# A decoder block on one core: the attention gate's modulation sums in an earlier stage, latent kv and q by token tile and half, and q's squares summed on ScalarE

## The chip, the core and the metric

The kernel runs on one core of a Trainium2 chip. The core has TensorE (PE, matrix products, with its weight loads as PEld), VectorE (DVE), ScalarE (ACT), GpSimd (POOL), SyncE (SP, which issues most loads), and 16 DMA engines. Each engine takes its instructions in the order in which the built program has them. The metric is the time of one execution on the device, in microseconds, the median of several runs.

## What is computed

One hybrid decoder block on 512 tokens of 1024 channels, in float32. A conditioning vector c gives six modulation vectors; h is the normed and modulated input; one wide product with `w_in` feeds two attention branches (latent attention, MLA, and native sparse attention, NSA) and two merge gates; then a merge, an output product and a SwiGLU mixer.

```
mod = silu(c) @ ada_w + ada_b                      # six vectors of 1024
sh1, sc1, gt1, sh2, sc2, gt2 = split(mod, 6)
h = rms_norm(x, norm1_gain) * (1 + sc1) + sh1
z = h @ w_in                                       # c_q, c_kv, k_pe, q_n, k_c, v_c, ..., gates
q  = rms_norm(c_q, q_a_gain) @ w_q_b               # 768 -> 8 heads x 96
kv = rms_norm(c_kv, kv_a_gain) @ w_kv_b            # 256 -> 8 heads x (64 + 64)
q, k = rms_norm over each head's 96, rope on the last 32
y_mla = causal_attention(q, k, v) @ w_o_mla
y_nsa = nsa_attention(...) @ w_o_nsa
x = x + gt1 * ((sigmoid(g_mla) * y_mla + sigmoid(g_nsa) * y_nsa) @ w_out)
h2 = rms_norm(x, norm2_gain) * (1 + sc2) + sh2
x = x + gt2 * ((silu(h2 @ w_gate) * (h2 @ w_up)) @ w_down)
```

The attention branch's gate modulation is gt1.

## The kernel before, in words

**Products in pieces.** A float32 product is made of three faster ones: each operand is split into a high and a low part (`hi_of` on ScalarE, `lo_of` on VectorE or GpSimd), and high x high, high x low and low x high are added in PSUM. A slab of weights goes through `wchunk`: a load by SP into `raw`, then `whi` on ScalarE and `wlo` on VectorE, four buffers of each.

**Stages.** The times are those of the profile, from the span's start. First `first_gemm`: it sums the modulation of sh1 and sc1 from strips of `ada_w` (tile `araw`), transposes and modulates x, and multiplies the first columns of `w_in` (to about 61 us). Then `segb2` (`gemm_wide`, eight slabs of 536 columns, tiles wa and wb) and `sega` (three `gemm_tok` of 352 columns, tile ga) multiply the next columns (to about 152). Beside them `weave` sets `prep`, a chain of small steps: q and k of the sparse branch are normed, turned and split (UQ, UK, sqq, pq, pk), and its compressed keys are made (X, FF, FS, cmp_w). Then the sparse attention (to about 290), with the merge gates' products (tile gp) as filler; then the stage here called the head projection (about 292 to 350); then the loop over the eight MLA heads (to about 447), then `y_mla`, the output product and the mixer.

**The head projection.** `latent_cols` transposes the latent rows in zA into cT, in a high and a low part. Two `gemm_tok` of `w_kv_b` (tile gk, 512 columns each, four heads a half) and two of `w_q_b` (tile gq, 384 columns) follow. `gemm_tok` holds the four token tiles in four PSUM buffers and finishes all of them at its end; the next one reuses the four. `use_kv` squares, copies and splits; the last token tile of a half norms k. `use_q` squares a tile on ScalarE into jq, copies it to qn, ropes it on VectorE, and sums jq's squares there by a reduction to msq. `norm_q` turns msq into the scale rsq, its iterations on GpSimd.

**The heads.** `mla_heads` transposes one head of qn and kn (tile pt) and splits them into qh, ql, kh, kl. `mla_scores` makes four score tiles ps (two PSUM buffers) and reduces each on VectorE, with the row minimum mn; ScalarE takes the exponential; VectorE scales. `mla_values` transposes the probabilities s, splits them into phi and plo, and multiplies with VM into av.

**Later modulations.** `mods` is a generator for gt1, sh2, sc2 and gt2. A half (512 channels) takes four strips of 512 KB; each strip's load is one step, and its two sums on VectorE (macc; the first of a half is a plain product) the next. So a half is eight steps. The half before is finished some steps later: two row halves of gt1 and gt2 by a product with ones (tile pm), a bias loaded into the row (gt), an addition, and for gt1 a halving on ScalarE. A strip lies in a buffer of `raw`, or, if `strip_src` holds a pool, in that pool's one buffer `strip`. `Side` hands out steps: eight in the head projection (`E_MODS`) and eight in the head loop (`F_MODS`), sixteen in all, then more in the stages behind.

**Who sets the order.** The program text gives an order, a scheduler at build time moves instructions of each engine where dependences allow it, and `pace` and `gate` add a few orders for fillers. So the engines' order of before and after is read from the built programs.

Of the kernel before, what the change touches and what calls it, by code (L numbers as in the profile page):

```python
# [28 lines left out]
WARM = 18  # L29
BRIDGE = 6  # L30
# [12 lines left out]
E_MODS = 8  # L43
F_MODS = 8
# [71 lines left out]
def hybrid_block(ctx, tc, a, out):  # L116
# [481 lines left out]
    w_in = a["w_in"][0]  # L598
    tab_st = scope()
# [338 lines left out]
    def latent_stats(pool_):  # L938
        for t in range(NT):
# [19 lines left out]
    segb2 = gemm_wide(hA, w_in, KD, SEG_B + 768, 280, 256, use_w, use_s, pair_first=True)  # L959
    pq, pk = prep_q(), prep_k()  # L960
    K, V = (0, "k"), (1, "v")
    prep = chain(compress_blocks(*K), part(pq, 5), compress_w1(*K), part(pq, 4), compress_w2(*K), compress_blocks(*V),
                 compress_out(*K), pq, compress_w1(*V), part(pk, 5), compress_w2(*V), pk, compress_out(*V), prep_gates())
    weave(segb2, prep, 1, 1)
    sega = chain(*[gemm_tok(hA, w_in, KD, SEG_A + c0, 352, use_a(c0), tag=f"a{c0}") for c0 in (0, 352, 704)])
    weave(sega, prep, 2, 1)
    run(prep)
    cp_st.close()
    zb_st.close()

    spilled = [dr.tile([4, P, S], F32, name=f"spill{i}") for i in range(6)]

    def turned_mm(ps, cols, A, h, l, first, last):
        for i, o in enumerate(ps):
            c = slice(cols + i * P, cols + (i + 1) * P)
            pe.matmul(o, h[:, c], A[0], start=first, stop=False)
            pe.matmul(o, h[:, c], A[1], start=False, stop=False)
            pe.matmul(o, l[:, c], A[0], start=False, stop=last)

    spill_src = {}  # L980

    def spill(ps, at, gate=None):
        if "pool" in spill_src:
            gs = spill_src["pool"].tile([P, S], F32, name="gs", tag="gs", bufs=spill_src["bufs"])
        else:
            gs = wp.tile([P, 1024], F32, name="gs", tag="raw")[:, :S]
        if gate is None:
            act.activation(out=gs, in_=ps, func=AF.Tanh, scale=0.5)
            act.dma_start(out=spilled[at // 4][at % 4], in_=gs)
        else:  # L990
            dve.scalar_tensor_tensor(out=gs, in0=gate, scalar=1.0, in1=ps, op0=ALU.add, op1=ALU.mult)
            pool.dma_start(out=spilled[at // 4][at % 4], in_=gs)

    def ahead(jobs, lead=1, eng=lambda: ()):
        ready = [wchunk(*job, *eng()) for job in jobs[:lead]]
        for i in range(len(jobs)):
            if i + lead < len(jobs):
                ready.append(wchunk(*jobs[i + lead], *eng()))
            yield ready.pop(0)

    def gates():
        jobs = [(rows(w_in, 0, KD, SEG_C + c, P), KD, P) for c in range(0, 2 * D, P)]
        for i, (h, l) in enumerate(ahead(jobs, FILL_LEAD, fill_lo)):
            ps = mm.tile([P, S], F32, name="gp", tag="mm")
            for k in range(KD):
                turned_mm([ps], 0, hT[k], h[:, k, :], l[:, k, :], k == 0, k == KD - 1)
                if k == KD - 1:
                    spill(ps, i)
                yield

    def y_nsa():
        jobs = [(rows(a["w_o_nsa"][0], 0, 4, c, 256), 4, 256) for c in range(0, D, 256)]
        for i, (h, l) in enumerate(ahead(jobs, FILL_LEAD, fill_lo)):
# [814 lines left out]
```

## Time and profile before

| | |
|---|---|
| median of three runs | 881.77 us (880.79 to 883.82) |
| the profiled execution's own time | 879.25 us |
| its span, first to last instruction | 877.5 us |
| mean granted TensorE clock | 0.989 |
| busy: PE, PEld, DVE, ACT, POOL | 842.3, 739.0, 677.2, 454.2, 122.0 us |
| DMA moved | 115.53 MB, mean 132 GB/s |

The profile is of one execution. A row of the windows gives a stretch, its length, then for PE, PEld, DVE, ACT and POOL the busy time and in brackets the number of instructions, the granted TensorE clock, the mean busy share of the DMA engines, and GB/s. A row of the waits names who waited for whom, the total, the number of times and the longest. A row of the timeline gives start, length, engine, operation, result and operands, shape and count, and in square brackets the idle time ahead of it and what ended that. Line 152 is that of a helper through which all engines' calls pass, so the rows are told apart by tile names. The end of a matrix product is modelled and products overlap, so starts are compared with starts.

### The profile page before, as it was taken

How to read it: one execution, taken by the hardware profiler on the slowest of the kernel's cores; microseconds unless marked ns; L12 is line 12 of the kernel's file. 1: busy time of each engine (PE TensorE's matmuls, PEld its weight loads, DVE VectorE, ACT ScalarE, POOL GpSimd, SP SyncE). 2: the span in 40 equal slices, each digit the busy share in tenths (PEclk: the TensorE clock that was granted, in tenths of full speed). 3: DMA queues.
4: the chain of work that ended last, by engine and by line, in shares of the span. 5: the costliest groups of instructions: out<-in, count | busy, mean ns of one | idle time of the engine just before them, and what ended most of it. 6: DMA issues, size and time to landing. Idle time of an engine off the chain costs nothing.

```text
span 877.5 us, 13876 instructions
## 1 busy us (share of the span) xinstructions
PE 842.3 (96%) x5028; PEld 739.0 (84%) x5028; DVE 677.2 (77%) x1400; ACT 454.2 (52%) x906; POOL 122.0 (14%) x203
## 2 busy tenths in 40 slices
PE   8899999889999998899899999999999999999997
PEld 6789899668777697688688889898999889988996
DVE  5788796887876689578879876986887759865875
ACT  4646564786765655466534264542465326641550
POOL 0005145343432025012200000000000000000000
PEclk9999999999999999799999999999999999999999
DMA  9944554221102456126497752453233413333312
GB/s 311 301 145 135 162 146 125 61 73 37 61 12 70 156 159 206 58 65 199 147 329 265 258 167 75 144 163 102 73 96 114 127 49 103 115 121 95 97 49 96
DMA packets 95704, 115.53 MB, mean 132 GB/s; under 512 B 6564, under 2 KB 68884, under 8 KB 95636
## 3 DMA queue, kind: packets, MB, share of 16 engines
q1 hardware_dynamic: 92596, 108.32, 40.2%
q10 hardware_dynamic: 2400, 4.23, 1.3%
q0 software_dynamic: 640, 2.10, 0.6%
q8 instruction: 39, 0.64, 0.3%
q14 instruction: 29, 0.24, 0.1%
HBM read 106.24 MB, written 8.39 MB: 131 GB/s over the span
## 4 chain that ended last, share of the span: by engine, by line
PE 47%; DVE 6%; DMA 3%; issue 1%; ACT 1%; DVEq 0%; ACTq 0%
PE d L152 14%; PE fx L152 11%; PE fy L152 8%; PE gwo L152 3%; PE gym L152 3%; PE wo L152 3%; DMA strip<-in_ada_w_dram 2%; PE gp L152 1%; DVE wlo L152 1%; DMA spill<-gs 1%; PE pt L152 1%; DVE macc L152 1%; PE fg L152 1%; DVE s L152 1%; PE fu L152 1%
## 5 line engine op out<-in xcount | busy, mean ns | idle before, releaser
L152 ACT ACTIVATE whi<-raw 128x1024 fp32r<-128x1024 f32 (+4 forms) x161 | 141.2, 893 | 144.0 <-PE d L152 44.0
L152 DVE TENSOR_TENSOR wlo<-raw,whi 128x1024 fp32r<-128x1024 f32 (+4 forms) x138 | 149.3, 1089 | 63.5 <-ACT whi L152 63.2
L152 PE MATMUL d<-wlo,mh 128*128 128x512 f32 (+1 forms) x180 | 70.2, 390 | 0.0
L152 PE MATMUL d<-whi,mh 128*128 128x512 f32 (+1 forms) x180 | 69.7, 392 | 0.6 <-DVE tm L152 0.5
L152 ACT ACTIVATE s<-s,mn 128x384 f32<-128x384 f32 (+2 forms) x96 | 52.6, 548 | 28.8 <-DVE mn L152 25.9
L152 PE MATMUL d<-whi,ml 128*128 128x512 f32 (+1 forms) x180 | 67.3, 389 | 0.0
L152 DVE TENSOR_TENSOR plo<-pt,phi 128x512 fp32r<-128x512 f32 (+2 forms) x78 | 46.2, 601 | 19.4 <-ACT phi L152 19.0
L152 PE MATMUL gp<-hTh,whi 128*128 128x512 f32 x128 | 54.5, 426 | 1.1 <-ACT qn L152 1.1
L152 ACT ACTIVATE phi<-pt 128x512 fp32r<-128x512 f32 (+2 forms) x78 | 40.0, 526 | 27.9 <-PE pt L152 27.2
L152 PE MATMUL gp<-hTh,wlo 128*128 128x512 f32 x128 | 51.0, 399 | 0.0
L152 PE MATMUL gp<-hTl,whi 128*128 128x512 f32 x128 | 50.8, 397 | 0.0
L152 ACT ACTIVATE whi<-s 128x1024 fp32r<-128x1024 f32 (+1 forms) x36 | 30.1, 845 | 30.7 <-PE d L152 18.0
L152 PE MATMUL fx<-h2h,whi 128*128 128x256 f32 x144 | 41.3, 287 | 0.0
L152 PEld LDWEIGHTS d<-whi,mh 128*128 128x128 f32 x180 | 33.7, 188 | 8.8 <-DVE tm L152 1.2
L152 PE MATMUL fx<-h2h,wlo 128*128 128x256 f32 x144 | 40.9, 284 | 0.1
L152 PE MATMUL fx<-h2l,whi 128*128 128x256 f32 x144 | 40.8, 284 | 0.0
L152 PEld LDWEIGHTS d<-whi,ml 128*128 128x128 f32 x180 | 33.8, 188 | 7.7
L152 PEld LDWEIGHTS d<-wlo,mh 128*128 128x128 f32 x180 | 33.8, 188 | 7.3
L152 DVE TENSOR_TENSOR wlo<-s,whi 128x1024 fp32r<-128x1024 f32 (+1 forms) x36 | 33.7, 950 | 7.6 <-ACT whi L152 7.4
L152 DVE SCALAR_TENSOR_TENSOR macc<-raw,csil,macc 128x512 f32<-128x512 f32 x45 | 33.6, 755 | 6.4 <-DMA raw<-in_ada_w_dram 6.2
L152 PE MATMUL pt<-ident,s 128*128 128x128 f32 x232 | 37.5, 280 | 0.2
L152 POOL TENSOR_TENSOR wlo<-raw,whi 128x512 fp32r<-128x512 f32 x24 | 31.1, 1320 | 27.6 <-ACT whi L152 27.5
(432 smaller groups left out, 2659.6 us busy)
## 6 DMA issues: line engine op xcount, KB each, us to landing
raw<-in_ada_w_dram SPq DMA_DIRECT2D x26, 512.0 KB, 4.4
raw<-in_ffn_w_gate_dram SPq DMA_DIRECT2D x22, 512.0 KB, 3.8
raw<-in_ffn_w_up_dram SPq DMA_DIRECT2D x22, 512.0 KB, 4.3
raw<-in_ffn_w_down_dram SPq DMA_DIRECT2D x22, 512.0 KB, 3.8
araw<-in_ada_w_dram SPq DMA_DIRECT2D x32, 256.0 KB, 6.2
raw<-in_w_in_dram SPq DMA_DIRECT2D x16, 512.0 KB, 5.1
raw<-in_w_in_dram SPq DMA_DIRECT2D x12, 352.0 KB, 3.1
x<-in_x_dram SPq DMA_DIRECT2D x8, 512.0 KB, 4.7
```

Of the source, the lines that this page charges most:

```text
L152: out = call(*args, **kw)
```

## The change

- `mods` is started ahead of `segb2`. A new wrapper `with_mods` takes its steps during `segb2` (every third step) and `sega` (every sixth), sixteen in all, with strips in a pool `ep` of one buffer. `E_MODS` and `F_MODS` become 0. The pool of macc and gt, `mcp`, is opened before the first stage.
- The head projection goes by token tile and half: `tok_major` finishes one token tile at a time in one PSUM buffer, `chunks` fetches the slabs apart from the products, and the order is kv first half, q first half, kv second half, q second half, with the heads 0 and 1 turned during the last. `mla_heads` is taken out of the head loop for these two, and is otherwise as it was.
- `use_q` copies the tile first and then squares each head apart, with ScalarE's accumulator giving the sum; the reduction on VectorE goes.
- The products that keep TensorE's clock up at the start are twice as many and half as wide.

```
-WARM = 18
-BRIDGE = 6
+WARM = 36
+BRIDGE = 12
...
-E_MODS = 8
-F_MODS = 8
+E_MODS = 0
+F_MODS = 0
...
-    heat = cst.tile([P, S], F32R, name="heat")
+    heat = cst.tile([P, 256], F32R, name="heat")
...
-            pe.matmul(o, heat[:, 0:P], heat, start=True, stop=True, skip_group_check=True)
+            pe.matmul(o[:, 0:256], heat[:, 0:P], heat, start=True, stop=True, skip_group_check=True)
...
+    mods_gen = mods()
+    mods_begun = []
...
+    ep_st = scope()
+    strip_src["pool"] = ep_st.enter_context(tc.tile_pool(name="ep", bufs=1, reuse_waits="tile"))
+
+    def with_mods(main, every):
+        for i, _ in enumerate(main):
+            if i % every == 0:
+                later(mods_gen, 2 if mods_begun else 1)
+                mods_begun.append(i)
+            yield
+
-    weave(segb2, prep, 1, 1)
+    weave(with_mods(segb2, 3), prep, 1, 1)
...
-    weave(sega, prep, 2, 1)
+    weave(with_mods(sega, 6), prep, 2, 1)
     run(prep)
+    later(mods_gen, 1)
+    ep_st.close()
+    strip_src.clear()
...
+        def chunks(w, kt, c0, n, got):
+            for k0 in range(0, kt, 2):
+                got.append(wchunk(rows(a[w][0], k0 * P, 2, c0, n), 2, n))
+                yield
+
+        def tok_major(off, kt, n, got, consume, tag):
+            for t in range(NT):
+                ps = mm.tile([P, S], F32, name=f"g{tag}{t}", tag="mm")[:, :n]
+                for k in range(kt):
+                    ah, al = (v[:, t * P : (t + 1) * P] for v in cT[off + k])
+                    h, l = (v[:, k % 2, :] for v in got[k // 2])
+                    pe.matmul(ps, ah, h, start=(k == 0), stop=False)
+                    pe.matmul(ps, ah, l, start=False, stop=False)
+                    pe.matmul(ps, al, h, start=False, stop=(k == kt - 1))
+                    if k % 3 == 2:
+                        yield
+                consume(t, ps)
+                yield
+
+        wk, wq = [[], []], [[], []]
+        kv_chunk = lambda c: chunks("mla_w_kv_b", 2, 512 * c, 512, wk[c])
+        q_chunks = lambda c: chunks("mla_w_q_b", 6, 384 * c, 384, wq[c])
+        run(kv_chunk(0))
         run(latent_cols(6, 7))
...
-                act.activation(out=jq, in_=pv, func=AF.Square)
                 act.activation(out=qn[t][:, hs, :], in_=pv, func=AF.Copy)
+                for h in range(4):
+                    act.activation(out=jq[:, h], in_=pv[:, h], func=AF.Square, accum_out=msq[:, c, t, h : h + 1])
...
-                dve.tensor_reduce(out=msq[:, c, t, :], in_=jq, axis=AX.X, op=ALU.add)
...
-        side.start(2 * 7 + 2 * 8, (gates_gen, E_GATES), (mods_gen, E_MODS))
-        for c in range(2):
-            with_side(mix((gemm_tok(sel_ct(6), a["mla_w_kv_b"][0], 2, 512 * c, 512, use_kv(c), tag=f"k{c}"), 5), (part(q_cols, 3), 3)))
+        side.start(4 + 6 + 3 + 12 + 1 + 7 + 12 + 4, (gates_gen, E_GATES), (mods_gen, E_MODS))
+        with_side(mix((tok_major(6, 2, 512, wk[0], use_kv(0), "k0"), 4), (q_cols, 6), (q_chunks(0), 3)))
...
-        for c in range(2):
-            with_side(gemm_tok(sel_ct(0), a["mla_w_q_b"][0], 6, 384 * c, 384, use_q(c), tag=f"q{c}"))
-            if c == 0:
-                run(norm_q(0))
+        with_side(mix((tok_major(0, 6, 384, wq[0], use_q(0), "q0"), 12), (kv_chunk(1), 1)))
+        run(norm_q(0))
+        with_side(mix((tok_major(6, 2, 512, wk[1], use_kv(1), "k1"), 4), (q_chunks(1), 3)))
+        qk = [[] for _ in range(NH)]
+        with_side(mix((tok_major(0, 6, 384, wq[1], use_q(1), "q1"), 12), (chain(mla_heads(0, qk[0]), mla_heads(1, qk[1])), 4)))
...
-        side.start(12 * NH, (chain(gates_gen, yn_gen), F_FILL), (mods_gen, F_MODS))
-        with_side(mla_heads(mat, 0, qk[0]))
-        with_side(mix((mla_scores(mat, 0, qk[0], sl[0]), 5), (mla_heads(mat, 1, qk[1]), 2)))
+        side.start(12 * NH - 4, (chain(gates_gen, yn_gen), F_FILL), (mods_gen, F_MODS))
+        with_side(mla_scores(mat, 0, qk[0], sl[0]))
```

In the built program the moved sums stand on VectorE among the low halves of `segb2` and the steps of `prep`, the strips' loads stand on SP between those of `w_in` and of the compression weights, and the two bias loads of gt1 stand on SP among the strips of the first stage. The products on TensorE in `segb2` and `sega` keep nearly their order, with one product pm added.

More of the change, by code (lines that the diff above doesn't have):

```diff
@@ L966, in hybrid_block @@
-    weave(sega, prep, 2, 1)
[L967 to L1009, printed above, removed]
@@ L1011, in y_nsa @@
-    def y_nsa():
-        jobs = [(rows(a["w_o_nsa"][0], 0, 4, c, 256), 4, 256) for c in range(0, D, 256)]
-        for i, (h, l) in enumerate(ahead(jobs, FILL_LEAD, fill_lo)):
-            for j in range(2):
-                ps = mm.tile([P, S], F32, name="yn", tag="mm")
-                at = 2 * i + j
-                gate = spill_src["pool"].tile([P, S], F32, name="gx", tag="gx", bufs=1)
-                sp.dma_start(out=gate, in_=spilled[2 + at // 4][at % 4])
-                for k in range(4):
-                    turned_mm([ps], j * P, (on_h[k], on_l[k]), h[:, k, :], l[:, k, :], k == 0, k == 3)
-                    if k == 3:
-                        spill(ps, 16 + at, gate)
-                    yield
@@ new lines, in hybrid_block, with turned_mm, spill @@
+    zb_st.close()
+    spilled = [dr.tile([4, P, S], F32, name=f"spill{i}") for i in range(6)]
+    def turned_mm(ps, cols, A, h, l, first, last):
+        for i, o in enumerate(ps):
+            c = slice(cols + i * P, cols + (i + 1) * P)
+            pe.matmul(o, h[:, c], A[0], start=first, stop=False)
+            pe.matmul(o, h[:, c], A[1], start=False, stop=False)
+            pe.matmul(o, l[:, c], A[0], start=False, stop=last)
+    spill_src = {}
+    def spill(ps, at, gate=None):
+        if "pool" in spill_src:
+            gs = spill_src["pool"].tile([P, S], F32, name="gs", tag="gs", bufs=spill_src["bufs"])
+        else:
+            gs = wp.tile([P, 1024], F32, name="gs", tag="raw")[:, :S]
+        if gate is None:
+            act.activation(out=gs, in_=ps, func=AF.Tanh, scale=0.5)
+            act.dma_start(out=spilled[at // 4][at % 4], in_=gs)
+        else:
+            dve.scalar_tensor_tensor(out=gs, in0=gate, scalar=1.0, in1=ps, op0=ALU.add, op1=ALU.mult)
+            pool.dma_start(out=spilled[at // 4][at % 4], in_=gs)
@@ new lines, in ahead, with gates @@
+    def ahead(jobs, lead=1, eng=lambda: ()):
+        ready = [wchunk(*job, *eng()) for job in jobs[:lead]]
+        for i in range(len(jobs)):
+            if i + lead < len(jobs):
+                ready.append(wchunk(*jobs[i + lead], *eng()))
+            yield ready.pop(0)
+    def gates():
+        jobs = [(rows(w_in, 0, KD, SEG_C + c, P), KD, P) for c in range(0, 2 * D, P)]
+        for i, (h, l) in enumerate(ahead(jobs, FILL_LEAD, fill_lo)):
+            ps = mm.tile([P, S], F32, name="gp", tag="mm")
+            for k in range(KD):
+                turned_mm([ps], 0, hT[k], h[:, k, :], l[:, k, :], k == 0, k == KD - 1)
+                if k == KD - 1:
+                    spill(ps, i)
+                yield
@@ new lines, in y_nsa @@
+    def y_nsa():
+        jobs = [(rows(a["w_o_nsa"][0], 0, 4, c, 256), 4, 256) for c in range(0, D, 256)]
+        for i, (h, l) in enumerate(ahead(jobs, FILL_LEAD, fill_lo)):
+            for j in range(2):
+                ps = mm.tile([P, S], F32, name="yn", tag="mm")
+                at = 2 * i + j
+                gate = spill_src["pool"].tile([P, S], F32, name="gx", tag="gx", bufs=1)
+                sp.dma_start(out=gate, in_=spilled[2 + at // 4][at % 4])
+                for k in range(4):
+                    turned_mm([ps], j * P, (on_h[k], on_l[k]), h[:, k, :], l[:, k, :], k == 0, k == 3)
+                    if k == 3:
+                        spill(ps, 16 + at, gate)
+                    yield
@@ L1227, in hybrid_block @@
         q_cols = latent_cols(*range(6))
-        def sel_ct(off):
-            return lambda k, t: (cT[off + k][0][:, t * P : (t + 1) * P], cT[off + k][1][:, t * P : (t + 1) * P])
         msq = mt.tile([P, 2, NT, 4], F32, name="msq")
```

48 lines of the change are left out of this document (25 added, 23 removed).

## The prediction

> **What bounds the kernel now.** I read the page first, then the stages in windows, then who waits in the stages that the change touches.
>
> ```profile
> span 877.5 us, 13876 instructions
> PE 842.3 (96%) x5028; PEld 739.0 (84%) x5028; DVE 677.2 (77%) x1400; ACT 454.2 (52%) x906; POOL 122.0 (14%) x203
> PEclk9999999999999999799999999999999999999999
> ```
>
> TensorE is busy for 96% of the span and none of its work leaves. So the change can win only time in which TensorE stands idle or runs slowly. The one dip of the clock lies in the seventeenth slice, about 351 to 373 us. The next view gives busy time by stage (stretch, its length, then PE, PEld, DVE, ACT, POOL, granted clock, DMA share, GB/s).
>
> ```profile
> 60.00:115.00 55.00, 52.37 (x378) 50.24 (x376) 42.81 (x92) 31.77 (x62) 14.92 (x24) 1.00 0.48 140
> 325.00:350.00 25.00, 21.78 (x123) 20.07 (x123) 24.93 (x76) 14.15 (x31) 11.38 (x22) 1.00 0.68 198
> 350.00:364.00 14.00, 11.66 (x37) 8.90 (x36) 9.20 (x25) 6.11 (x18) 1.88 (x4) 0.51 0.31 98
> 337.98:359.69 21.71, 16.15 (x72) 12.58 (x71) 18.32 (x57) 12.54 (x32) 8.51 (x23) 0.78 0.57 173
> ```
>
> From 325 to 350 us, the second half of the q projection and the head transposes, VectorE is full (24.93 of 25) and TensorE loses 3.2 us. Right behind it TensorE runs at half clock for 14 us. The TensorE waits of this region (total, times, longest) and the instructions at the turn say why.
>
> ```profile
> PE ps L152 <- DVE mn L152: 3.2, 3, 2.1
> PE gk L152 <- ACT whi L152: 1.2, 1, 1.2
> PE gk L152 <- DVE wlo L152: 0.4, 1, 0.4
> PE gp L152 <- ACT qn L152: 1.1, 1, 1.1
> ```
> ```profile
> 337.98 0.60 PE L152 MATMUL pt<-ident,qn 128*96 128x128 f32 x4
> 349.59 0.45 PE L152 MATMUL ps<-kh,qh 96*128 96x384 f32 x1 [2.10 <-DVE mn L152]
> 359.69 0.79 PE L152 MATMUL av<-phi,VM 128*128 128x512 f32 x1 [1.21 <-ACT phi L152]
> ```
> ```profile
> 347.96 1.30 DVE L152 TENSOR_TENSOR wlo<-raw,whi 128x512 fp32r<-128x512 f32 x2
> 349.18 0.34 DVE L152 CUSTOM_DVE_ANT_0 s<-ps,mask,rsq 128x128 f32<-128x128 f32 x1
> ...
> 351.74 0.75 DVE L152 CUSTOM_DVE_ANT_0 s<-ps,mask,rsq 128x512 f32<-128x512 f32 x1 [0.65 <-PE ps L152]
> ```
>
> The third score product waits 2.10 us because VectorE reaches the first score tile only at 349.18, after a backlog. I call 337.98 to 359.69, from the end of the q projection to the first value product, the turn: 21.71 us, of which TensorE is busy 16.15, and much of that at half clock.
>
> **The change part by part.** First what leaves VectorE. The rows are the groups of VectorE from 296 to 350 us (count, busy us, mean ns, idle before).
>
> ```profile
> L152 DVE SCALAR_TENSOR_TENSOR macc<-raw,csil,macc 128x512 f32<-128x512 f32 x12 | 9.0, 752 | 3.2 <-DMA raw<-in_ada_w_dram 3.2
> L152 DVE TENSOR_REDUCE msq<-jq 128x4 f32<-128x384 f32 x8 | 4.3, 539 | 0.0
> L152 DVE TENSOR_SCALAR macc<-raw,csil 128x512 f32<-128x512 f32 x2 | 1.0, 478 | 0.0
> ```
>
> Of the sixteen sums fourteen ran here: 9.0 + 1.0 = 10.0 us, with 3.2 us of standing for their strips; the reductions were 4.3. VectorE loses 14.3 us of work and 3.2 us of waits just where it was full. ScalarE pays for the reductions: per token tile one 384-wide square (about 0.49 us) becomes four 96-wide ones, each followed by an accumulator read. No 96-wide one is in the trace; these neighbours bound it.
>
> ```profile
> 168.47 0.41 ACT L152 ACTIVATE jk<-zA 128x256 bf16<-128x256 f32 x1
> 168.78 0.20 ACT L152 ACTIVATION_READ_ACCUMULATOR jk<-zA 128x1 f32 x1
> 169.26 0.22 ACT L152 ACTIVATE jk<-zA 128x32 bf16<-128x32 f32 x1
> 169.38 0.20 ACT L152 ACTIVATION_READ_ACCUMULATOR jk<-zA 128x1 f32 x1
> 169.47 0.59 ACT L152 ACTIVATE phi<-pt 128x512 fp32r<-128x512 f32 x1
> ```
>
> Start to start, 32 columns take 0.12 us, 256 take 0.31 and the read 0.09. By columns 96 take about 0.17, so a head is 0.26 and a tile 1.05; eight tiles add 8 x (1.05 - 0.40) = 5.2 us to ScalarE, which was busy 14.15 of 25 in that window. The upper end takes shown durations one after another: (0.41 + 0.20) x 4 = 2.44 a tile.
>
> Next the order. ScalarE at the end of the q projection, before:
>
> ```order
> L152 ACTIVATE qh<-pt,cols_712 96x512
> L152 ACTIVATE kh<-pt,cols_712 96x512
> L152 ACTIVATE jq<-gq_3974 128x384
> L152 ACTIVATE qn_3510<-gq_3974 128x384
> L152 ACTIVATE qh<-pt,cols_712 96x512
> L152 ACTIVATE kh<-pt,cols_712 96x512
> L152 ACTIVATE whi<-raw 128x512 x2
> L152 ACTIVATE gs<-gp 128x512
> ```
>
> And now (gq is a token tile's q product, qh and kh are a head's turned operands, s the scores):
>
> ```order
> L152 ACTIVATE qn_3577<-gq_4130 128x384
> L152 ACTIVATE jq,msq<-gq_4130 128x96 x4
> L152 ACTIVATE qh<-pt,cols_739 96x512
> L152 ACTIVATE whi<-raw 128x512 x4
> L152 ACTIVATE qn_3578<-gq_4169 128x384
> L152 ACTIVATE jq,msq<-gq_4169 128x96 x4
> L152 ACTIVATE whi<-raw 128x512 x2
> L152 ACTIVATE kh<-pt,cols_739 96x512
> L152 ACTIVATE s_4229,sm<-s_4229,mn 128x128
> ```
>
> Three of the four head operands are now made ahead of the last product's end; the turn keeps 24 score products, 24 gate products, 4 head transposes and 7 of the probabilities. TensorE's floor comes from the steps below.
>
> ```profile
> 340.94 0.40 PE L152 MATMUL gp<-hTh,whi 128*128 128x512 f32 x1
> 341.17 0.39 PE L152 MATMUL gp<-hTl,whi 128*128 128x512 f32 x1
> 338.42 0.60 PE L152 MATMUL pt<-ident,kn 128*96 128x128 f32 x4
> ```
>
> 512 columns step by 0.23 us; four transposes by 0.44 (337.98 to 338.42). So 24 x 0.23 = 5.5; two heads of 3 x 1280 columns, 3.5; eleven transposes 1.2: together 10.2 us, the lower end. The other chain is ScalarE's last tile (0.4 + 1.05), two slab halves and VectorE's low halves (about 1.7), then eight score reductions of 0.34 to 0.75 by width, 4.4 for two heads, about 2.5 (an estimate) for the last operand and the scaling, and 1.2 to the first value product as shown. That is 11.3. The score tiles are two deep, so the chains don't overlap fully: I take 12.5. The twelve transposes that moved into the projection cost 1.3 there. Gain at the turn: 21.7 - 12.5 - 1.3 = 7.9 us. The full clock is part of it. At 0.51 the 11.66 us of busy TensorE in 350 to 364 held at most 5.7 us too much, a part of it under waits for VectorE; I take 4.5, so that a turn in which the clock halves again takes about 17.
>
> The clock first by its row: 0.51 over 350 to 364, behind a longest wait of 2.10. The Trainium skill (TensorE: Matmul & The Clock Gate, Part 1) says that half rate comes after an idle window of about 3.4 us, and full rate after one busy window of that length. The trace differs in both: 2.10 us of idling among short products was enough, and the return took four such windows. By the page a lone fall would cost about 1.7 us, by the row 4 to 5; the sum uses the row.
>
> At the start of this stage the first kv slab is fetched and split ahead of the latent transposes, so the two waits on whi and wlo, 1.2 + 0.4, should go. ScalarE is then crowded in the first quarter (four transposed latents beside the kv tiles), and I take 0.8 of it as lost again. Net 0.8, ends -1 and +1.6. In the head loop nothing else leaves VectorE: its later sums belong to the next modulation and stay; only one finished half-row moves out. I take 0.5, ends 0 and 1.5.
>
> Now what arrives earlier. Sixteen sums are 14 x 0.75 + 2 x 0.48 = 11.5 us on VectorE, all of them between 57 and 109 us. There it has 55.0 - 42.8 = 12.2 us idle in 60 to 115. The waits in that stage:
>
> ```profile
> DVE wlo L152 <- ACT whi L152: 7.8, 6, 4.4
> ```
> ```profile
> 87.99 0.66 PE L152 MATMUL pq<-ident,UQ 128*128 128x128 f32 x4 [1.20 <-POOL UQ L152]
> 94.63 0.43 PE L152 MATMUL ga<-wlo,hTh 128*128 128x352 f32 x1 [1.39 <-DVE wlo L152]
> ```
> ```profile
> raw<-in_ada_w_dram SPq DMA_DIRECT2D x26, 512.0 KB, 4.4
> ```
>
> VectorE between the second sum of the first strip and the first of the next one, now:
>
> ```order
> L152 SCALAR_TENSOR_TENSOR macc<-strip,csil,macc 128x512
> L152 COPY ZC_213<-wb_230 128x256
> L152 COPY ZC_214<-wb_230 128x256
> L152 COPY cols_739<-pt 128x50
> L152 SCALAR_TENSOR_TENSOR trig<-trig 128x120
> L152 TENSOR_TENSOR wlo<-raw,whi 128x536
> L152 TENSOR_SCALAR cols_739<-cols_739 64x1
> L152 SCALAR_TENSOR_TENSOR trig<-trig 128x120 x2
> L152 TENSOR_SCALAR trig<-trig 128x120
> L152 SCALAR_TENSOR_TENSOR trig<-trig 128x120
> L152 SCALAR_TENSOR_TENSOR macc<-strip,csil,macc 128x512
> ```
>
> Before, the same rows stood there without the two sums:
>
> ```order
> L152 COPY ZC_192<-wb_209 128x256
> L152 COPY ZC_193<-wb_209 128x256
> L152 COPY cols_712<-pt 128x50
> L152 SCALAR_TENSOR_TENSOR trig<-trig 128x120
> L152 TENSOR_SCALAR cols_712<-cols_712 64x1
> L152 SCALAR_TENSOR_TENSOR trig<-trig 128x120
> L152 TENSOR_TENSOR wlo<-raw,whi 128x536
> ```
>
> The strip has one buffer, so its load starts only behind the pair of sums ahead, and 4.4 us pass to landing; some 2.7 us of work stand between. VectorE then waits about 1.7 us at the head of its queue, and by my count of the rows so at four of the seven places: 6.8 us. Behind it stand the low halves that the products need. On SP the loads of w_in and of the compression weights wait behind the blocked strip, but for a buffer too. The scheduler has put the norm chain of q later, and slabs are split some chunks ahead, so I take 0.5 us lost at the wait of 94.63, ends -1 (the wait on UQ goes) and +4.
>
> The two loads of the gate's bias now stand amid the fourth group of strips of the very first stage, where the DMA engines are full:
>
> ```profile
> 2.50:40.00 37.50, 33.45 (x197) 28.57 (x197) 26.02 (x59) 19.06 (x34) 0.00 (x0) 1.00 1.07 350
> DMA to landing us min/median/max: 5.7/6.2/6.5
> 20.20 7.19 SPq L152 DMA_DIRECT2D araw<-in_ada_w_dram  x8
> 35.40 3.11 DVE L152 SCALAR_TENSOR_TENSOR acc<-araw,csil,acc 128x512 f32<-128x512 f32 x4
> ```
>
> 512 KB at 350 GB/s are 1.5 us. The last strip of that group is issued by 27.4 and lands by 33.6; its rows are summed from 35.4 on. The delay is covered: 0, and 1.5 without that cover. The heater's products are twice as many and half as wide, so the same columns: 0, ends -0.3 and +0.3.
>
> Sum: 7.9 + 0.8 + 0.5 - 0.5 = 8.7 us. The profiled execution took 879.25, 2.5 below the median of 881.77; the gain goes off both: 870.5 for a like execution, 873.0 for the median.
>
> **The rivals.** The clock falls again. The turn still has short score products between waits, and the threshold isn't known from one dip. Then it takes 17 in place of 12.5: 877.5. For it: 2.10 us were enough. Against it: VectorE's backlog of 14.3 us is gone.
>
> ScalarE becomes the bound of the q projection. At 2.44 + 0.49 a tile plus two operands and six slab halves (about 4.5) its last quarter takes 4 x 2.93 + 4.5 = 16.2 us against TensorE's 72 products at 0.17, 12.2: 4 us late, 877. Against it: the overlapped steps above.
>
> The strips hold VectorE. The Trainium skill (TensorE: Matmul & The Clock Gate, the section on the array as 16 sub-arrays) says that VectorE's queue is strictly first in, first out. The trace agrees as far as the sums go: VectorE stood 3.2 us for their strips. Of its 12.2 us idle, 7.8 were waits for ScalarE's whi; if those can't be filled, 4.4 are left for 11.5 of sums, and 7.1 + 6.8 = 13.9 us fall on the low halves. It decides once VectorE is later than the slabs are ahead. Then the median is 873.0 + 13.9 - 0.5, about 886, slower than before.
>
> **How the numbers follow.** Forecast 0.62, 873.0. Clock 0.16, 877.5. ScalarE 0.07, 877. Strips 0.08, 886. A rest of 0.07 has gains that cancel against a milder strip wait, about 881. My own range for the forecast goes from the lower end of the turn (10.2 for 12.5) with the waits at the stage's start and in the head loop wholly gone and nothing lost early, 873.0 - 2.3 - 0.8 - 1.0 - 1.5 = 867.4, to 3 us lost early, 876. Taking in the clock and ScalarE gives 867 to 879. A measurement here tells about 0.3%, 2.6 us, from no change; below 879.1 counts as faster. Faster 0.62 + 0.16 + 0.07 = 0.85, same 0.07, slower 0.08.
>
> **What would show it.** Right: no dip of the granted clock near 340 to 365; the turn near 12.5 us; no third score product waiting 2 us; VectorE below 90% ahead of it; the accumulator reads on ScalarE stepping by 0.09. Wrong: new waits of TensorE on wlo between 60 and 115, or sums waiting for strips there by more than 7 us with the products late; the first group of products later than 62 us would mean that the bias loads weren't covered. If the turn is short and the time is not, what was won came back early.

## The result and the profile after

The changed kernel took 876.07 us (median of 20 runs, 872.5 to 881.56), the kernel before 882.65 us beside it (20 runs, 879.19 to 887.53). The ratio is 0.9925, 95% interval 0.9906 to 0.9943: 6.6 us faster. The profiled execution took 874.82 us.

The head of the page: busy time of each engine and the granted clock in 40 slices.

```profile
span 873.0 us, 13961 instructions
PE 841.4 (96%) x5052; PEld 740.4 (85%) x5052; DVE 668.7 (77%) x1392; ACT 457.2 (52%) x962; POOL 119.2 (14%) x203
PEclk9999799999999999999999999999999999999999
```

The dip of the clock has left the seventeenth slice, and one has come into the fifth, about 87 to 109 us. The windows that the prediction showed of before, now (stretch, length, PE, PEld, DVE, ACT, POOL, granted clock, DMA share, GB/s); the last row is the turn, from the first score product to the first value product.

```profile
60.00:115.00 55.00, 48.55 (x339) 46.98 (x338) 45.15 (x99) 28.10 (x55) 17.29 (x24) 0.91 0.62 192
325.00:350.00 25.00, 23.99 (x134) 21.84 (x133) 20.80 (x69) 19.73 (x79) 6.34 (x25) 1.00 0.35 94
350.00:364.00 14.00, 11.69 (x60) 9.09 (x59) 11.56 (x33) 9.08 (x24) 5.14 (x14) 1.00 0.46 151
347.40:361.25 13.85, 11.54 (x61) 9.10 (x60) 11.72 (x38) 10.66 (x35) 5.15 (x14) 1.00 0.42 134
```

VectorE went from 24.93 to 20.80 of 25 us, and the turn is at full clock. (The stage runs about 9.4 us later now; in the stretch that lies to it as 325 to 350 did before, 334.4 to 359.4, VectorE is busy 19.64.) In the first row TensorE is busy 48.55 of 55 us where it was 52.37, at a clock of 0.91. The waits of that stretch, 60 to 115 us (total, times, longest):

```profile
DVE macc L152 <- DMA strip<-in_ada_w_dram: 8.6, 5, 2.1
...
ACT sqq L152 <- DVE msq L152: 5.4, 3, 3.6
...
PE pq L152 <- POOL UQ L152: 3.2, 1, 3.2
PE ph L152 <- DVE gn L152: 3.2, 1, 3.2
```

VectorE at that place, in order of time (idle time ahead of a row in brackets), shows how these four belong together. The first block is of before, the second of the changed kernel, and the third has the two waits of TensorE there.

```profile
76.41 0.69 DVE L152 TENSOR_REDUCE msq<-sqq 128x8 f32<-128x512 f32 x1
...
88.22 0.17 DVE L152 COPY gn<-wa 128x24 f32<-128x24 f32 x1
```

```profile
83.19 0.89 DVE L152 SCALAR_TENSOR_TENSOR macc<-strip,csil,macc 128x512 f32<-128x512 f32 x1 [1.77 <-DMA strip<-in_ada_w_dram]
84.01 1.34 DVE L152 TENSOR_TENSOR wlo<-raw,whi 128x1024 fp32r<-128x1024 f32 x1
85.27 0.81 DVE L152 SCALAR_TENSOR_TENSOR macc<-strip,csil,macc 128x512 f32<-128x512 f32 x1
86.00 0.68 DVE L152 TENSOR_REDUCE msq<-sqq 128x8 f32<-128x512 f32 x1
...
90.53 0.65 DVE L152 TENSOR_SCALAR macc<-strip,csil 128x512 f32<-128x512 f32 x1 [1.91 <-DMA strip<-in_ada_w_dram]
91.10 2.30 DVE L152 TENSOR_TENSOR wlo<-raw,whi 128x1024 fp32r<-128x1024 f32 x1
93.32 0.80 DVE L152 SCALAR_TENSOR_TENSOR macc<-strip,csil,macc 128x512 f32<-128x512 f32 x1
94.04 0.67 DVE L152 TENSOR_REDUCE msq<-sqq 128x8 f32<-128x512 f32 x1
94.75 0.29 DVE L152 TENSOR_TENSOR V<-wa,V 128x128 fp32r<-128x128 f32 x1
94.96 0.17 DVE L152 COPY gn<-wa 128x24 f32<-128x24 f32 x1
```
```profile
90.95 1.11 PE L152 MATMUL pq<-ident,UQ 128*128 128x128 f32 x4 [3.24 <-POOL UQ L152]
95.28 0.55 PE L152 MATMUL ph<-whi,FS 128*128 128x256 f32 x1 [3.21 <-DVE gn L152]
```

The sums of squares of q (msq) stand behind strip sums: eight of the sixteen come ahead of the first, at 86.00 for 76.41. ScalarE has one buffer for q's squares (sqq) and waits for each msq, GpSimd waits for sqq, and TensorE's transposes of q (pq) wait for GpSimd's UQ. The copies out of the second segment's product (V, gn), too, stand behind a strip sum, and the compressed keys' products (ph) wait for them.

Where the time lies, from the starts of named products in the two profiled executions:

| start of | before | after | difference |
|---|---|---|---|
| the third segment (first ga) | 92.49 | 101.23 | +8.74 |
| its last product | 150.23 | 157.97 | +7.74 |
| the sparse branch's last pair of score products | 265.86 | 275.79 | +9.93 |
| the first MLA value product | 359.69 | 361.25 | +1.56 |
| the last one | 446.46 | 443.65 | -2.81 |
| the mixer's first product | 515.46 | 512.67 | -2.79 |
| the program's last product | 873.38 | 868.92 | -4.46 |

So the head stages win 8.4 us up to the first value product and 4.4 in the loop, 12.7 together, and 9.9 are lost ahead of them. Of these 9.9, 7.7 are there at the end of the third segment. The other 2.2 come in the sparse attention, where the clock is halved from 171.74 to 178.56 in this execution and nowhere in that of before. That may be the execution and not the change: ten of the twelve profiles of the experiments below show such falls between 156 and 197 us, among them e1, e9 and e10, whose third segment runs as before. The last step, from -2.79 to -4.46, is a dip of the clock behind 517 us that the profile of before has and that of the changed kernel hasn't. The two executions differ by 4.4 us and the medians by 6.6: the profiled execution of before, 879.25 us, lies 3.4 under its median, that of the changed kernel 1.3 under its own.

### The profile page after: what moved, and what is told of

It is laid out like the page before. It is cut to its first block, busy times and chain, and to the rows that moved or that the text cites. A ratio compares the mean times of both kernels' runs of the same rounds, so it can differ in the third digit from the quotient of the medians.

```text
span 873.0 us, 13961 instructions
## 1 busy us (share of the span) xinstructions
PE 841.4 (96%) x5052; PEld 740.4 (85%) x5052; DVE 668.7 (77%) x1392; ACT 457.2 (52%) x962; POOL 119.2 (14%) x203
## 4 chain that ended last, share of the span: by engine, by line
PE 79%; DVE 8%; DMA 7%; ACT 3%; issue 2%; SPq 1%; ACTq 0%; DVEq 0%
PE d L152 14%; PE fx L152 12%; PE gp L152 9%; PE fy L152 9%; PE pt L152 4%; DMA strip<-in_ada_w_dram 4%; PE av L152 3%; PE ga L152 3%; PE gwo L152 3%; PE gym L152 3%; PE fg L152 3%; PE yn L152 3%; PE wo L152 3%; PE gq L152 2%; PE fu L152 2%
## 5 line engine op out<-in xcount | busy, mean ns | idle before, releaser
L152 PEld LDWEIGHTS pt<-ident,s 128*128 128x128 f32 x232 | 28.1, 142 | 7.6 <-issue 2.1
```

What stands on the lines that cost most here:

```text
L152: out = call(*args, **kw)
```

## Experiments

My theory at this point: the head stages win because VectorE is rid of the sums, and the early stage loses because these sums delay what stands behind them on VectorE. Rivals: the win is that of the new order of the head projection, or of the loads that went with the sums; the early loss is that of the single strip buffer, or of the half clock.

The kernel before ran beside each of three groups of experiments (medians 882.48, 882.62 and 884.4 us), so kernels are compared by their ratio to the one that ran beside them.

| kernel | median us | ratio, 95% interval |
|---|---|---|
| changed | 876.07 | 0.9925, 0.9906 to 0.9943 |
| e1 sums late | 878.01 | 0.9945, 0.9923 to 0.9966 |
| e2 sums early, old order | 875.85 | 0.9938, 0.9910 to 0.9966 |
| e3 square and reduction | 876.55 | 0.9926, 0.9902 to 0.9950 |
| e4 two strip buffers | 874.88 | 0.9921, 0.9892 to 0.9949 |
| e5 sums after q | 872.24 | 0.9873, 0.9841 to 0.9905 |
| e6 three early, five later | 871.86 | 0.9880, 0.9853 to 0.9907 |
| e7 sums after q, old order | 877.71 | 0.9947, 0.9925 to 0.9969 |
| e8 bare loads | 877.06 | 0.9929, 0.9905 to 0.9953 |
| e9 no sums | 871.33 | 0.9851, 0.9816 to 0.9887 |
| e10 no sums, old order | 872.85 | 0.9876, 0.9844 to 0.9909 |
| e11 six and two | 874.32 | 0.9902, 0.9867 to 0.9938 |
| e12 heat in the wait | 877.24 | 0.9927, 0.9896 to 0.9959 |

And by stage, from one profiled execution each: start and end of the third segment, and the length of the head stages from the sparse branch's last pair of score products to the last value product.

| kernel | third segment | head stages |
|---|---|---|
| before | 92.49 to 150.23 | 180.6 |
| changed | 101.23 to 157.97 | 167.9 |
| e1 | 92.83 to 150.56 | 176.9 |
| e2 | 100.59 to 157.51 | 168.7 |
| e3 | 100.29 to 156.91 | 170.9 |
| e4 | 100.09 to 157.62 | 169.3 |
| e5 | 93.17 to 155.62 | 168.3 |
| e6 | 96.49 to 152.80 | 169.3 |
| e7 | 93.32 to 153.20 | 172.0 |
| e8 | 99.94 to 156.70 | 168.3 |
| e9 | 92.69 to 150.83 | 168.9 |
| e10 | 92.71 to 150.87 | 173.7 |
| e11 | 92.89 to 150.25 | 172.3 |
| e12 | 98.21 to 159.94 | 169.6 |

**e1, sums late.**

```
-E_MODS = 0
-F_MODS = 0
+E_MODS = 8
+F_MODS = 8
...
-    weave(with_mods(segb2, 3), prep, 1, 1)
+    weave(segb2, prep, 1, 1)
...
-    weave(with_mods(sega, 6), prep, 2, 1)
+    weave(sega, prep, 2, 1)
```

> The changed kernel (876.1 us) with the sixteen sums back where they were, eight steps in the head projection and eight in the head loop; the new order of the head projection and the squares on ScalarE stay. My theory: of the two parts, the early sums cost about 8.7 us between 87 and 101 us (two waits of TensorE of 3.2 us and 10 us at half clock behind them), and the head stages win 13.2 us, some two thirds of it through the new order. Then the early 8.7 come back and about 4 to 5 are lost in the head stages: about 872, with the first product of the third segment at 92 to 93 us as before. Rival one, the win in the head stages is VectorE's relief by the sums and not the order: then most of the 13.2 is lost and 8.7 come back, 880 to 881. Rival two, the early waits have nothing to do with the sums: the early stage stays at 101 us and the time rises to 880 or more.

Measured 0.9945. The early loss is gone (92.83), so rival two falls, and the head stages take 176.9 in place of 167.9: 9 of the 12.7 us are the sums, more than I gave them. The time, 878.0, lies between my 872 and the 880 of rival one. The score products at the turn, after:

```profile
351.46 0.44 PE L152 MATMUL ps<-kh,qh 96*128 96x384 f32 x1 [1.79 <-DVE mn L152]
355.21 0.44 PE L152 MATMUL ps<-kh,qh 96*128 96x128 f32 x1 [1.22 <-DVE mn L152]
```

The waits for the row minimum are back with the sums, in the new order too, and so is the half clock (353 to 363 us). The new order by itself, with the sums where they were, is worth 0.55% of the kernel before, 4.9 us (interval 3.0 to 6.8).

**e2, sums early, old order.**

```
-        with_side(mix((tok_major(6, 2, 512, wk[0], use_kv(0), "k0"), 4), (q_cols, 6), (q_chunks(0), 3)))
+        for c in range(2):
+            with_side(mix((gemm_tok(sel_ct(6), a["mla_w_kv_b"][0], 2, 512 * c, 512, use_kv(c), tag=f"k{c}"), 5), (part(q_cols, 3), 3)))
...
+                act.activation(out=jq, in_=pv, func=AF.Square)
...
-                for h in range(4):
-                    act.activation(out=jq[:, h], in_=pv[:, h], func=AF.Square, accum_out=msq[:, c, t, h : h + 1])
...
+                dve.tensor_reduce(out=msq[:, c, t, :], in_=jq, axis=AX.X, op=ALU.add)
```

> The changed kernel with the sums early, but the head projection in the order of before (latent kv both halves, then q both halves, heads turned behind it) and one square with a reduction on VectorE. My theory (two thirds of the win in the head stages is the order and the squares): the early loss of 8.7 stays and 4 to 5 of 13.2 are won, so 882.6 + 8.7 - 4.5 = about 887. Rival one (VectorE's relief is the win): about 877 to 879. Rival three, nothing in the head stages can be had without both parts: 890 or more.

Measured 0.9938, and not above the kernel before: rival one holds. With the old order the head stages take 168.7 us, within 1 us of the changed kernel, and VectorE is as free as there:

```profile
325.00:350.00 25.00, 24.94 (x144) 24.42 (x143) 18.61 (x61) 11.72 (x24) 7.45 (x29) 1.00 0.45 127
```

So the two parts overlap: the sums alone are worth 11.9 us of head stages (e2 against before), the order alone 3.7 (e1 against before), both 12.7.

**e3, the squares alone.** The same two lines on the squares as in e2, in the changed kernel.

> The changed kernel with q's squares as before: one 384-wide square on ScalarE and a reduction on VectorE. By the prediction ScalarE saves 8 x 0.65 = 5.2 us and VectorE gets 4.3 us more in the head projection. If VectorE has room there now (20.8 of 25 us busy) and ScalarE too (19.7 of 25): no difference, 875 to 877. If VectorE's relief counts further: 878 to 880. If ScalarE is what the first value product waits for: 873 to 874.

Measured 0.9926, as the changed kernel: no difference that can be told. VectorE took 22.72 of 25 us in 325 to 350 for 20.80, ScalarE 15.68 for 19.73; both have room now.

**e8, the loads alone.**

```
+    def bare_loads():
+        for hf in range(2):
+            for r0 in range(0, KD, 2):
+                raw = wp.tile([P, 1024], F32, name="raw", tag="raw")
+                sp.dma_start(out=raw.rearrange("p (r n) -> p r n", r=2), in_=rows(ada, r0 * P, 2, 2 * D + hf * S, S))
+                yield
+                yield
```

> The kernel with early sums and the old order of the head projection (875.9), to which the eight strip loads of the head stages are given back as bare loads into the shared raw buffers, with no sums on them (they add 4 MB and change no result). Theory, VectorE's 10 us of sums and its 3.2 us of standing for strips are what the head stages lose by: 876 to 878, the turn without a wait of 2 us. Rival, it is the loads, which take a raw buffer from the slabs and the DMA engines in the projection: 881 or more, with TensorE waiting for whi or wlo of the slabs or VectorE full again by late low halves.

Measured 0.9929 with head stages of 168.3 us, no worse than e2. The loads as such cost nothing there, so what the head stages lost by were the sums on VectorE, its 10 us of work or its standing still for strips; which of the two isn't taken apart. One thing this run doesn't test: a bare load gives its buffer back when it has landed, a strip that is summed holds it until the sum is done.

**e4, two strip buffers.**

```
-    heat = cst.tile([P, 256], F32R, name="heat")
+    heat = cst.tile([P, 224], F32R, name="heat")
...
-            return strip_src["pool"].tile([P, 1024], F32, name="strip", tag="strip", bufs=1)
+            return strip_src["pool"].tile([P, 1024], F32, name="strip", tag="strip", bufs=strip_src.get("bufs", 1))
...
+    strip_src["bufs"] = 2
```

> The changed kernel with two strip buffers in the early stage (and the clock-keeping products of the first stage 224 instead of 256 columns wide, to make room). My theory: VectorE stood 8.6 us at the head of its queue for strips because the next load could start only behind the sums; with a second buffer the loads run ahead, these waits nearly go, q's sums of squares and the copies that free the product's buffers come in time, and TensorE's two waits of 3.2 us shrink below 1.5 us, with no half clock behind them: about 869. Rival: it is the 11.5 us of sums themselves on a full VectorE that push these rows back, not the waits for strips: 875 to 877, the two waits as long as now.

Measured 0.9921, the rival's result. One long wait of TensorE took the place of two. VectorE stood less for strips in all, 5.2 us in 60 to 115 for 8.6, though its longest wait grew:

```profile
93.31 0.90 PE L152 MATMUL pq<-ident,UQ 128*128 128x128 f32 x3 [5.99 <-POOL UQ L152]
```
```profile
83.77 0.75 DVE L152 SCALAR_TENSOR_TENSOR macc<-strip,csil,macc 128x512 f32<-128x512 f32 x1 [3.18 <-DMA strip<-in_ada_w_dram]
```
```profile
DVE macc L152 <- DMA strip<-in_ada_w_dram: 5.2, 3, 3.2
```

With more buffer the scheduler put more sums ahead of q's squares: 14 ahead of the first msq, for 8. The waits for strips shrank by 3.4 us and the third segment starts only 1.1 earlier, so my theory of the blocked buffer falls as the main cause. What counts is which rows stand behind the sums. As the order changed with the buffer, what the buffer is worth by itself isn't shown.

**e6, a hole for q.**

```
+    dve.pace = 1
     weave(with_mods(sega, 6), prep, 2, 1)
+    dve.pace = 0
```

> The changed kernel with three strips summed before 82 us as now, and the other five held on VectorE behind the rows of the third segment's products at which they stand in the program text; none between the squares of q and the copies out of the product's buffers. My theory: the waits of 3.2 us at 91 and 95 us and the half clock behind them go, and the later sums fit into VectorE's gaps at 105 to 115 and 135 to 150 us: about 869. Rival one (the waits come from elsewhere): 876 with both waits still there. Rival two: the sums only move the loss, into the scores of the sparse branch at 158 to 175 us, where VectorE's row minimum is waited for: 873 to 876, with the waits there longer than now.

Measured 0.9880, 0.45% below the changed kernel; the two intervals just touch (0.9907 and 0.9906). One of the two waits went, one stayed, and the third segment starts at 96.49:

```profile
90.73 0.66 PE L152 MATMUL pq<-ident,UQ 128*128 128x128 f32 x4 [3.17 <-POOL UQ L152]
```

Three early strips alone still push the compressed keys and q's squares back by 4 to 5 us (the first square of q starts at 80.68, before at 75.75). The time, 871.9, lies between my 869 and the 873 of rival two, of which a part came true: a wait of 1.85 us for the key rows at 155 us is new.

**e5, all sums after q.** As in e6 with the wrapper around `segb2` taken off, `with_mods(sega, 3)` and a pace of 32.

> The changed kernel (876.1 us) with all sixteen sums held on VectorE behind the copies out of the second segment's products, spread over the third segment (97 to 150 us) and clear of the sparse branch's first scores. So far: two strip buffers did not help (874.9; the wait for UQ grew to 6.0 us), three strips early and five late gave 871.9 with a wait of 3.2 left. My theory now: the sums, not the waits for their strips, push back the compressed keys and the squares of q that stand behind them on VectorE; with none ahead of them the third segment starts near 92.5 us as before, and 8 us of 8.7 come back: 867 to 869. Rival one: that much VectorE work in the third segment delays the low halves or the sparse branch's start, and the last product of the segment comes later than 152 us: 871 to 874. Rival two, the early loss was not the sums: 876.

Measured 0.9873; the intervals of this kernel and the changed one just don't meet (0.9905 and 0.9906). The start of the third segment is that of before (93.17), which shows that the sums made the early loss. Its end isn't (155.62): rival one. TensorE's waits there are for low halves (before had one, of 1.39), each followed by 3.4 us at half clock:

```profile
96.12 0.43 PE L152 MATMUL ga<-wlo,hTh 128*128 128x352 f32 x1 [2.30 <-DVE wlo L152]
...
121.18 0.44 PE L152 MATMUL ga<-wlo,hTh 128*128 128x352 f32 x1 [1.23 <-DVE wlo L152]
```

**e7, the same with the old order.** e2's head projection in e5.

> As the run before in this list (sums in the third segment), with the head projection in the order of before and one square with a reduction on VectorE. The sums early with the old order gave 875.9, no worse than the changed kernel. If the new order and the squares on ScalarE are worth nothing once the sums are gone: the same time as the run before within 0.3%, 867 to 869. If they win the 4 us that they won with the sums still there (878.0 against 882.5): 871 to 873. If they cost: 865 or less.

Measured 0.9947, 0.74% more than e5, so here the order is worth something, and more than any of the three expectations had. The profiled execution, 873.6 us and so 4 under the median, shows 3.7 us of it in the head stages (172.0 for 168.3), with 6.8 us at half clock at the turn. What the median adds to that isn't placed.

**e9 and e10, no sums at all.**

```
+                if slot == 4:
+                    dve.memset(acc, 0.0)
                 for r0 in range(0, KD, 2):
+                    if slot == 4:
+                        yield
+                        if r0 == MOD_LAG and late:
+                            finish_last(late)
+                        yield
+                        continue
```

> The changed kernel without the gate's sixteen sums and their eight strips: they are left out, macc is filled with zeros, and the rest is as in the changed kernel. It is the bound of what placing the sums better can give, with the new order of the head projection. My theory (the sums early cost what stands behind them on VectorE, 6 to 8 us; the head stages are as in the changed kernel): 867 to 869, the first product of the third segment at 92 to 93 us. Rival, sums in the third segment (872.2) were already free: 871 to 873.

> As the run before in this list (sums left out), with the order of the head projection and the square with its reduction as before. It tells what order and squares are worth by themselves. So far two pairs say 4.5 to 5.5 us (878.0 against 882.5 with the sums in the head stages, 872.2 against 877.7 with the sums in the third segment) and one says nothing (876.1 against 875.9 with the sums early). If the order is worth something whenever the rest leaves room: 872 to 874, with TensorE's half clock at the turn to the first value product. If it is worth nothing once VectorE is relieved: within 1.5 us of the run before.

Measured 0.9851 and 0.9876. Both kernels leave the gate's sums and their strips out, so what they compute isn't the block. e9's 871.3 us is the rival's time, not the 867 to 869 of my theory; e10's 872.9 fits both of its expectations. Without sums the third segment runs as before (92.69 to 150.83) and the head stages as in the changed kernel (168.9): the early loss and the late gain are both those of the sums. 0.9851 bounds what a better place for them can give; e5 and e6 are within 0.3% of it, which the intervals don't tell from nothing. In the profiles, though, the third segment of e5 ends 4.8 us later than that of e9, so something may be left there. The two kernels differ by 0.25%, and the intervals overlap. In all four pairs (before and e1, e2 and changed, e7 and e5, e10 and e9) the new order is on the faster side, by 0.55, 0.13, 0.74 and 0.25%. In the first and the third pair the difference is clear of the intervals, in the other two it isn't. So the order is worth something between nothing and 6.5 us, by what stands beside it; why it counts more in one place than in another isn't shown.

**e11, six strips in the third segment, two in the head loop.** As e5 with `with_mods(sega, 4)`, a pace of 34 and `F_MODS = 4`.

> A placement made from the runs so far: six strips (twelve sums) in the third segment, the first of them behind its first low halves, and the last two strips in the head loop. With all eight in the third segment the time was 872.2 and TensorE waited 2.3 and 1.2 us for low halves at 96 and 121 us. Theory: fewer sums there leave the low halves in time and the head loop has room for four: 869 to 871. Rival, four sums in the head loop bring back waits for the row minimum there: 872 to 874.

Measured 0.9902 and 874.3 us, just above the rival's 872 to 874. Twelve sums in the third segment cost nothing there (92.89 to 150.25), but the first of the four in the head loop fell into the turn. TensorE, then VectorE at that place:

```profile
346.40 0.44 PE L152 MATMUL ps<-kh,qh 96*128 96x384 f32 x1 [1.30 <-DVE mn L152]
352.24 0.39 PE L152 MATMUL ps<-kh,qh 96*128 96x256 f32 x1 [3.37 <-DVE mn L152]
```
```profile
347.77 0.08 DVE L152 DVE_READ_ACCUMULATOR2_ANT mn<- 128x1 f32 x1
350.76 0.75 DVE L152 SCALAR_TENSOR_TENSOR macc<-raw,csil,macc 128x512 f32<-128x512 f32 x1 [2.90 <-DMA raw<-in_ada_w_dram]
351.43 0.74 DVE L152 CUSTOM_DVE_ANT_0 s<-ps,mask,rsq 128x512 f32<-128x512 f32 x1
```

One sum that stands 2.90 us for its strip at the head of VectorE's queue holds the score tiles behind it, and TensorE waits 3.37. The last two strips in yet another place weren't tried.

**e12, heat in the wait.**

```
+        if i == 0:
+            keep_clock(tp.tile([P, S], F32, name="warm", tag="tp"), 52)
+            warm_last = pe.last
...
+                if i == 0 and k0 + j == 0:
+                    pe.follow(pe.last, warm_last)
```

> The changed kernel with 52 clock-keeping products (5.9 us at full clock) put on TensorE where it waited between the second segment and the compressed keys' products, 87 to 95 us. They compute nothing that is used. Theory: the half clock from 89.8 to 100.0 came of the idle windows there; with TensorE busy the products for the compressed keys (32 of them, 5.95 us at half clock, 3.95 at full in the kernel before) run at full clock and the third segment starts about 2 us earlier, at 99 us: 873 to 875. Rival one, the clock falls in any case: 876. Rival two, the products delay what follows them by more than the clock gives: 877 or more.

Measured 0.9927, as the changed kernel, and by its 877.2 us rival two. The first half of the theory holds: 32 products for the compressed keys took 3.98 us for 5.96 (94.23 to 98.21), and the third segment starts 3.0 us earlier. But it ends 2.0 later. The first row below is the heat; the last is the wait that came:

```profile
87.12 6.39 PE L152 MATMUL warm<-heat 128*128 128x256 f32 x52
94.23 0.36 PE L152 MATMUL ph<-whi,FS 128*128 128x256 f32 x1 [0.72 <-DVE gn L152]
...
101.64 0.66 PE L152 MATMUL ga<-wlo,hTh 128*128 128x352 f32 x1 [2.16 <-DVE wlo L152]
```

TensorE came earlier to low halves that VectorE hadn't made: the first product with one starts at 101.64, and at 101.72 in the changed kernel. So VectorE bounds this place, and the half clock ahead of it is mostly hidden under that. Behind the new wait the clock fell again, from 101.61 to 105.03, which costs up to 1.7 of the 2.0 us. The products of q, too, moved behind the heat (97.97 for 87.10), so a part may be theirs.

## Why the prediction was right, and where it was off

**The sign, the size and the range** held: 873.0 forecast, 876.07 measured, range 867 to 879. By parts two errors of opposite sign are in it: the head stages won 12.7 us where 9.2 were forecast, and the early stage lost 7.7 where 0.5 were. That the sum stayed in the range is luck in so far as these two partly cancel.

**The turn and the start of the stage.** Forecast 7.9 + 0.8; measured 8.4 from the last sparse score to the first value product. From the last product of the q projection to the first value product it was 21.88 us (337.81 to 359.69) and is 14.02 (347.23 to 361.25), 7.9 less. The forecast for that stretch alone was 9.2 less, to 12.5, which was 1.5 low; ahead of it 0.8 - 1.3 = -0.5 was forecast and 0.5 won (71.94 to 71.44 us from the last pair of sparse scores). So 8.4 for 8.7 holds two smaller errors that cancel. Most signs named for it are there: no dip at 340 to 365, VectorE at 20.80 of 25, the longest wait for the row minimum 0.57 us for 2.10:

```profile
354.89 0.39 PE L152 MATMUL ps<-kh,qh 96*128 96x256 f32 x1 [0.57 <-DVE mn L152]
...
361.25 0.50 PE L152 MATMUL av<-phi,VM 128*128 128x512 f32 x1 [1.59 <-ACT phi L152]
```

The cause was shared out wrongly between order and sums, though. Nor did all 14.3 us leave VectorE "just where it was full": of the fourteen sums six, 4.2 us, stood in 325 to 350, and the waits of 3.2 us for strips all came earlier. I built the 12.5 from the new order's list of steps; e2 reaches head stages within 1 us of it with the old order, and e1 shows that the sums are 9 of 12.7 us.

**The squares.** Forecast 0.26 us a head on ScalarE; a square and its read step by 0.22:

```profile
339.90 0.25 ACT L152 ACTIVATE jq<-gq 128x96 f32<-128x96 f32 x1
340.03 0.20 ACT L152 ACTIVATION_READ_ACCUMULATOR jq<-gq 128x1 f32 x1
340.12 0.25 ACT L152 ACTIVATE jq<-gq 128x96 f32<-128x96 f32 x1
```

ScalarE didn't become the bound, and e3 shows that the step bought nothing by itself once the sums were gone.

**The head loop.** Forecast 0.5, measured 4.4. About 2 of it is the tail of the half clock of before (359.69 to 363.86), which I had put into the turn. In the profile of e1, with the sums back and at full clock, the loop takes 83.82 us for 82.40, so about 1.4 of the rest may go with the sums; that is one execution of each.

**The early stage is the step that failed.** "I take 0.5 us lost at the wait of 94.63, ends -1 (the wait on UQ goes) and +4": measured 7.7 at the end of the third segment. The mechanism of the third rival was there, VectorE's queue held by strips, 8.6 us of standing for the 6.8 that I counted, and so was the sign named for being wrong: sums waiting for strips by more than 7 us with the products late. But its price was put on the wrong rows. I looked at the low halves behind the sums, which are split ahead, and took the later norm chain of q for a cover. That chain and the copies out of the finished product were what TensorE waited for next (pq 3.24 us, ph 3.21 us); for a low half it waited nowhere in 60 to 115. Of the 8.7 us at the start of the third segment 0.9 are there at the end of the second, 5.3 are these two waits (1.20 was there before), and 2.0 are the compressed keys' products at half clock (5.96 us for 3.95). e5, e9 and e11 show it: with no sums ahead of q the segment starts at 93.17, 92.69 and 92.89.

**The bias loads** cost nothing that shows: the first product of the first segment started at 14.34 and now at 14.19 us, and the second segment's last product is 0.9 later, with VectorE fuller in that stretch.

**The clock.** I wrote that 2.10 us of idling was enough and that the return took four windows. Cut into windows of 3.41 us that end where the clock fell, before shows why:

```profile
346.79:350.20 3.41, 1.31 (x7) 0.84 (x6) 3.15 (x10) 2.53 (x7) 2.75 (x9) 1.00 0.73 223
350.20:353.61 3.41, 3.09 (x12) 2.57 (x11) 1.66 (x6) 2.16 (x8) 0.30 (x2) 0.50 0.71 225
353.61:357.02 3.41, 2.59 (x8) 1.61 (x8) 2.95 (x8) 0.72 (x4) 0.69 (x1) 0.50 0.00 0
357.02:360.43 3.41, 2.20 (x9) 1.59 (x8) 2.49 (x9) 2.35 (x6) 0.71 (x1) 0.50 0.50 154
360.43:363.84 3.41, 3.41 (x12) 2.80 (x11) 2.09 (x4) 0.68 (x1) 0.00 (x0) 0.50 0.00 0
363.84:367.25 3.41, 3.41 (x21) 2.89 (x20) 0.75 (x2) 1.12 (x3) 0.00 (x0) 1.00 0.00 0
```

The clock halves behind a window in which TensorE was busy 1.31 us, stays so through three windows with waits in them, and comes back behind the first full one. In this fall that is closer to the Trainium skill (TensorE: Matmul & The Clock Gate, Part 1) than I made it: a free-running window of 3413 ns, and full rate after one busy window. What differs is the idle window, which need not be idle. And not every return came behind the first full window: in the changed kernel the fall at 171.74 lasted two windows, with TensorE busy 3.41 us in both. The rival of a second fall came about, but early in the kernel (89.8 to 100.1 us) and not at the turn. That none came at the turn is in part luck: e6 and e9, with the head stages of the changed kernel, show a fall of 3.4 us there (at 354.2 and 350.3).

## What to carry to other kernels

Work that is moved to an engine with idle time is paid for by the rows that stand behind it in that engine's queue: list these rows and who waits for them, down to chains over three engines, and not only the rows of the main product. When one change does several things, run each alone before crediting any: here the moved sums made both the gain and the loss, and the new order less than its list of steps promised. A place for all or most of such work behind the critical chain (e5, e6) came out at 872 us, against 876 and 882.6 for the two kernels.

## What the runs showed of the hardware

The granted clock falls in whole steps of 3.41 us. In the fourteen profiles it fell 41 times, the fall at each program's end left out, each time for one, two, three or four such windows (3.4, 6.8, 10.2 and 13.7 us), and the falls of one execution lie on one grid (before: 350.20 and 517.46, 49 windows apart). In the window ahead of a fall TensorE was busy 0 to 2.70 us. The less busy the window, the more often it was followed by a fall. Of the windows of this grid at full clock, all 16 with less than 1.5 us busy were, 12 of 30 with 1.5 to 2.0, 11 of 85 with 2.0 to 2.5, 2 of 149 with 2.5 to 3.0 and none of the 3176 above. The grid lies elsewhere in each execution, so the same wait falls into one window or is cut in two. The waits of 0.73 and 0.89 us at 515 to 517 us halved the clock in the profile of before, where both lie in a window with 1.80 us busy. In that of the changed kernel they lie in two windows, with 2.69 and 2.53 us busy, and the clock stayed. This goes with the spread of the runs: those of the changed kernel reach from 872.5 us at a mean clock of 0.993 to 881.56 us at 0.980.
